# Reciprocal roots moved from GpSimd to VectorE, and the first layer's x scaled half on VectorE

## The chip, the cores and the metric

The kernel runs on one core of one Trainium2 chip. The metric is the device time of one execution in microseconds. Three runs of the kernel before gave 1405.43, 1406.83 and 1408.57 us, median 1406.83. The core has a matmul engine (TensorE, PE in the rows; PEld is its weight load), VectorE (DVE), ScalarE (ACT), GpSimd (POOL) and SyncE (SP, which issues all loads).

## What is computed

A trunk of two layers over 256 latent tokens and 256 context tokens of width 1024. The lines that matter here, cut from the reference:

```python
def rmsnorm(x, g):
    xf = x.astype(jnp.float32)
    y = xf * lax.rsqrt(jnp.mean(xf * xf, axis=-1, keepdims=True) + EPS)
    return (y * g.astype(jnp.float32)).astype(x.dtype)
...
for l in range(DEPTH):
    h = rmsnorm(x, norm_g[l, 0]) * (1.0 + mod[:, 1]) + mod[:, 0]
    y, yc = mixer_sublayer(h, hc, ...)
    x = x + mod[:, 2] * rmsnorm(y, norm_g[l, 1])
    h = rmsnorm(x, norm_g[l, 2]) * (1.0 + mod[:, 4]) + mod[:, 3]
    x = x + mod[:, 5] * rmsnorm(conv_ffn(h, ...), norm_g[l, 3])
...
```

In layer 0 the context tokens take the same steps. The mixer has four branches (mLSTM, differential attention, Fourier, spatial gating) with merge gates and one output projection; the FFN is gated, with a convolution over tokens. Each norm needs one reciprocal root for each token.

## The kernel before

All matmuls work on values split in a high and a low part (`hi`, `lo`), three matmuls for each product. `wload` (line 111) loads a weight tile of 128x1024, ScalarE casts it to `hi` (line 122), and `lo = raw - hi` is made on VectorE in one instruction or on GpSimd in four pieces of 128x256 (line 131), alternating by a running fraction. These subtractions are most of GpSimd's work.

Layer 0 keeps activations with the features on the partitions, in two halves of 256 tokens (context and latent). After the output projection and after the FFN's last matmuls, each half goes through `chain` (line 327). A column sum of squares over the tokens stands in PSUM (`st`); VectorE makes the variance from it (`rs_v`, line 176); `rsqrt` (line 149) raises it to the power -0.5 with one GpSimd instruction on a 128x2 tile (`rs_y`, line 151); and `spread_rows` (line 179) turns it with matmuls into a tile `R` that holds one root per column, in PSUM (line 182). Then VectorE scales y by R (line 341), VectorE and GpSimd add it to x (line 343), squares of the new x are summed, and the second norm repeats the same steps up to `modulate` (line 297, lines 300 to 302), which makes the next sublayer's input. There are four chains (two sublayers, two halves), so eight such roots. A chain is a generator: `pump` runs a step of it between groups of matmuls.

In layer 1 only the latent tokens go on, and the mixer's output is made with tokens on the partitions (`TokOut`): four quarters, two of tokens `t` by two of features `d`. `take` squares a quarter on ScalarE (line 439) and multiplies it by the gate row: on VectorE from PSUM (line 442), but for the last quarter (t = d = 1) by a ScalarE copy and a GpSimd product (lines 444 and 445; bit 1 of `yp`). `residual` makes the root for one token tile (`rstd_tok`, line 419, a 128x1 tile) and updates x (line 453). `tok_h1` squares the new x (line 483), multiplies it by the next norm's row (line 484), makes another root, scales the identity with it (`dg`, line 487), and TensorE turns the tokens back with `dg` (line 493), after which `tok_h2` splits h for the FFN. At the end of the FFN `residual(t, True)` also stores the result.

At the start of layer 0 (`start`), the norm's root comes last: matmuls run on unscaled x while the modulation is still being computed, then `R` is spread, VectorE copies it to SBUF (`Rs`, line 628), and GpSimd multiplies the eight tiles `x0[k]` (128x512) by it (line 631, `xr`). Then `bmain` interleaves steps of the modulation: matmuls `ada` (line 209), a VectorE copy of their result (`ada_sb`, line 213), small matmuls on that copy (line 219), and `shifted`, which makes the shifted h that the other branches read: a ScalarE pass (line 586), a VectorE pass `t` (line 587) and the low part (line 588).

Every engine works in its own fixed order. That order is made ahead of time by a planner that takes instructions by priority (the order of the program, moved by `later` and `issue_after`) as their inputs become ready by its own costs.

Of the kernel before, what the change touches and what calls it, by code (L numbers as in the profile page):

```python
# [10 lines left out]
F32 = mybir.dt.float32  # L11
F32R = mybir.dt.float32r
I32 = mybir.dt.int32
AF = mybir.ActivationFunctionType
ALU = mybir.AluOpType
# [7 lines left out]
KF = 22  # L23
EPS = 1e-6
SEGS = ((0, 6), (6, 14), (14, 22))
CFG = dict(hi=4, raw=4, tb=0.6, tw=0.8, tw1=1.0, x1=2, mm=3, paddk=8, tk=4, acc=2, f3=(2, 2), qa=(0, 0), f0=(1, 1), f1=(1, 2), f2=(1, 2), n0=(1, 1), n1=(1, 1), hd=1, hq=3, na=48, tu=3, to=1, ka=2, yp=3, ph=400, kh=4, kt=4, ld=2, dl=2, W=2, h0=3, mix=1, keep=4, hot=400, nst=6, nb=1, pt=(1, 0), w1=14, w2=6, wd=(24,), ahead={7: (0, -1, 1), 0: (2,), 1: (3,)}, so=("mddddfddd", "mdpf", "mpf", "mrpfd0q"), xr="pppppppp", fw=(0, 2), g0="nddddddd", g1=("nddddddn", "nddddddn"), g3=("nddddddn", "ndndndnd"), gy="nddddddn", cm=1, h1=2, xp=2, pf=(1, 1), ck=1, ys=(1, 1, 1, 1), c0=1, te=0.8)

C_ID, C_MF, C_MB, C_RC, C_RS, C_SEL, C_ONE, C_END = 0, 128, 256, 384, 448, 512, 514, 515
F_DFT, F_CD, F_SD, F_ND, F_END = 0, 512, 640, 768, 896
# [6 lines left out]
def trunk_kernel(ctx: ExitStack, tc: tile.TileContext, I, out):  # L36
    nc = tc.nc
# [3 lines left out]
    lp = ctx.enter_context(tc.tile_pool(name="lp", bufs=1))  # L41
    rawp = ctx.enter_context(tc.tile_pool(name="rawp", bufs=CFG["raw"]))
    hip = ctx.enter_context(tc.tile_pool(name="hip", bufs=CFG["hi"]))
    lop = ctx.enter_context(tc.tile_pool(name="lop", bufs=CFG["hi"]))
    hp = ctx.enter_context(tc.tile_pool(name="hp", bufs=1))
    tiny = ctx.enter_context(tc.tile_pool(name="tiny", bufs=4))
    wk = ctx.enter_context(tc.tile_pool(name="wk", bufs=2))
    zap = ctx.enter_context(tc.tile_pool(name="zap", bufs=1))
    mmp = ctx.enter_context(tc.tile_pool(name="mmp", bufs=CFG["mm"], space=PSUM))
    axp = ctx.enter_context(tc.tile_pool(name="axp", bufs=8 - CFG["mm"], space=PSUM))  # L50
    drp = ctx.enter_context(tc.tile_pool(name="drp", bufs=2, space=bass.MemoryType.DRAM))
# [7 lines left out]
    def aux(name="aux"):  # L59
        return axp.tile([128, 512], F32, tag="aux", name=name)  # L60
# [7 lines left out]
    def keep_warm(n, prev, mid=False):  # L68

        if n:  # L70
            ps = mmb("warm") if mid else aux("warm")
            with after(prev):
                for _ in range(2 * n):
                    at = nc.tensor.matmul(ps[:, 0:256], still[:, 0:128], still, start=True, stop=True)
            prev = ins_of(at)
        return prev

    turn = [0.0, CFG["tb"]]
    todo = []
# [69 lines left out]
    def rsqrt(v, n):  # L149
        y = tiny.tile([128, 16], F32, tag="rs_y", name="rs_y")[:, :n]  # L150
        nc.gpsimd.tensor_tensor(out=y, in0=v, in1=mh[:, :n], op=ALU.pow)
        return y

    @contextmanager
    def later(n):
        p = tc.cur_priority
        tc.cur_priority = p + n
        yield
        tc.cur_priority = p + (tc.cur_priority - p - n)

    def after(i):
        return tc.issue_after(i) if i is not None else ExitStack()
# [7 lines left out]
            nc.tensor.matmul(st[:, t:t + 1], sq[:, t * 128:(t + 1) * 128], onec, start=(first and t == 0),  # L170
                             stop=last and t == n // 128 - 1)

    def rstd_rows(st, n, spread=True):
        nt = n // 128
        v = tiny.tile([128, 16], F32, tag="rs_v", name="rs_v")[:, :nt]
        nc.vector.tensor_scalar(out=v, in0=st[:, :nt], scalar1=1.0 / D, scalar2=EPS, op0=ALU.mult, op1=ALU.add)
        return spread_rows(rsqrt(v, nt), nt) if spread else rsqrt(v, nt)

    def spread_rows(r, nt):
        R = aux("R")  # L180
        for t in range(nt):
            nc.tensor.matmul(R[:, t * 128:(t + 1) * 128], r[:, t:t + 1].to_broadcast([128, 128]), ident,
                             start=True, stop=True)
        return R[:, :nt * 128]
# [111 lines left out]
    def modulate(h, k, xk, R, c0, c1, A, B, boff):  # L296
        n = c1 - c0
        s = 0 if c0 == 0 else 1
        u = wk.tile([128, 512], F32, tag="t1", name="t1")
        nc.vector.scalar_tensor_tensor(out=u[:, :n], in0=xk, scalar=A[:, k, s:s + 1], in1=R, op0=ALU.mult, op1=ALU.mult)  # L300
        nc.scalar.activation(out=h[k][0][:, c0:c1], in_=u[:, :n], func=AF.Identity, bias=B[:, boff + k, s:s + 1], scale=1.0)  # L301
        nc.vector.scalar_tensor_tensor(out=h[k][1][:, c0:c1], in0=u[:, :n], scalar=B[:, boff + k, s:s + 1],
                                       in1=h[k][0][:, c0:c1].bitcast(F32), op0=ALU.add, op1=ALU.subtract)
# [24 lines left out]
    def chain(yn, c0, c1, G, h, A, B, boff, plan):  # L328

        n = c1 - c0  # L330
        s = 0 if c0 == 0 else 1
        r = rstd_rows(yn.acc[c0].st, n, False)
        for _ in range(CFG["ys"][0]):
            yield

        R = spread_rows(r, n // 128)
        S = Stat(n, plan)
        S.late = []
        for k in range(KD):
            t = yn.y[k][:, c0:c1]  # L340
            nc.vector.scalar_tensor_tensor(out=t, in0=t, scalar=G[:, k, s:s + 1], in1=R, op0=ALU.mult, op1=ALU.mult)
            e = nc.gpsimd if k < CFG["paddk"] and k % 2 == 0 else nc.vector
            e.tensor_tensor(out=x[c0][k], in0=x[c0][k], in1=t, op=ALU.add)
            S.drop(CFG["ys"][2])
            S.add(k, x[c0][k])
            if k % CFG["ck"] == CFG["ck"] - 1:
                yield

        for _ in range(CFG["ys"][3]):
            yield  # L350
        S.drop(0)

        r = rstd_rows(S.st, n, False)
        for _ in range(CFG["ys"][1]):
            yield

        R = spread_rows(r, n // 128)
        for k in range(KD):
            modulate(h, k, x[c0][k], R, c0, c1, A, B, boff)
            if k % CFG["cm"] == CFG["cm"] - 1:  # L360
                yield
# [54 lines left out]
            g.append(gt)  # L416
        return g

    def rstd_tok(ss):
        v = tiny.tile([128, 16], F32, tag="rs_v", name="rs_v")[:, 0:1]  # L420
        nc.vector.tensor_scalar(out=v, in0=ss[:, 0:1], scalar1=ss[:, 1:2], scalar2=D * EPS, op0=ALU.add, op1=ALU.add)
        return rsqrt(v, 1)

    class TokOut:
        def __init__(self, grow):
# [21 lines left out]

        def residual(self, t, store=False):

            r = rstd_tok(self.ss[t])  # L450
            for d in range(2):
                xd = xt[t][:, d * 512:(d + 1) * 512]
                nc.vector.scalar_tensor_tensor(out=xd, in0=self.ys[t, d], scalar=r, in1=xd, op0=ALU.mult, op1=ALU.add)
                if store:
                    nc.sync.dma_start(out=out[t * 128:(t + 1) * 128, d * 512:(d + 1) * 512], in_=xd)
# [21 lines left out]
    def tok_h1(t, xa, arow, hb):  # L477

        ss = tiny.tile([128, 2], F32, tag="ss", name="ss")
        for d in range(2):  # L480
            jk = wk.tile([128, 512], F32, tag="sq", name="jk")
            xd = xt[t][:, d * 512:(d + 1) * 512]
            sq.append(nc.scalar.activation(out=jk, in_=xd, func=AF.Square, accum_out=ss[:, d:d + 1]))
            nc.vector.tensor_tensor(out=xa[t][:, d * 512:(d + 1) * 512], in0=xd, in1=arow[d], op=ALU.mult)
        r = rstd_tok(ss)
        dg = wk.tile([128, 512], F32, tag="t2", name="dg")[:, 0:128]
        hb["dg"] = nc.vector.tensor_scalar(out=dg, in0=ident, scalar1=r, scalar2=RS, op0=ALU.mult, op1=ALU.mult)
        for d in range(2):
            ps = aux("hT")
            for j in range(4):  # L490
                k = 4 * d + j
                with after(warmed[0]):
                    at = nc.tensor.matmul(ps[:, j * 128:(j + 1) * 128], xa[t][:, k * 128:(k + 1) * 128], dg,
                                          start=True, stop=True)
            hb[t, d] = ps
        if t == 0:
            warmed[0] = keep_warm(CFG["w2"], ins_of(at), True)
# [15 lines left out]
    def start(stp):  # L513
# [5 lines left out]
        x0 = [stp.tile([128, T], F32, name=f"x0{k}") for k in range(KD)]  # L519
# [8 lines left out]
        Rs = stp.tile([128, T], F32, name="Rs")  # L528
# [72 lines left out]
        S = Stat(T, CFG["g0"])  # L601
# [9 lines left out]
        nb, rs = CFG["nb"], []  # L611
# [13 lines left out]
            for c in CFG["so"][j]:  # L625
                steps[c]()
        r = rs[0]
        nc.vector.tensor_copy(Rs, spread_rows(r, 4))
        nc.vector.tensor_copy(idr, cst[:, C_ID:C_ID + 36])
        for k in range(KD):  # L630
            (nc.gpsimd if CFG["xr"][k] == "p" else nc.vector).tensor_tensor(out=x0[k], in0=x0[k], in1=Rs, op=ALU.mult)

        def bstep(i):
            bmain(nb + i)
# [13 lines left out]
    def layer(l):  # L648
# [15 lines left out]
        with ExitStack() as es:  # L664
# [23 lines left out]
            def hot():  # L688
                return later(-CFG["hot"] if last else 0)
# [933 lines left out]
def ins_of(i):  # L1623
    return i.ins if hasattr(i, "ins") else i
# [79 lines left out]
```

## Time and profile before

| | |
|---|---|
| median of three runs | 1406.83 us (1405.43 to 1408.57) |
| profiled execution, its own time | 1407.98 us |
| span of that execution | 1406.2 us |
| mean granted TensorE clock | 0.983 |
| busy: PE, PEld | 1336.9 us, 1195.1 us |
| busy: DVE, ACT, POOL | 863.8 us, 621.6 us, 849.7 us |

The busy time of an engine counts its instructions from start to end, so an instruction that is held up while it runs counts as busy. A line of the timeline gives the start, the time up to the end of the last of the merged instructions, the engine, the line of the kernel, the operation, the tiles (written tile first), the shapes and the count. In square brackets stands the idle time of the engine before it, and what ended it.

### The profile page before, as it was taken

What the parts mean: (1) busy time and instruction counts of PE and PEld (TensorE: products, weight loads), DVE (VectorE), ACT (ScalarE), POOL (GpSimd) and SP (SyncE); (2) the same over time, 40 slices, a digit from 0 to 9 for tenths busy, and PEclk for the clock granted to TensorE, in tenths of its full rate; (3) what the DMA queues carried; (4) which work ended last, traced back from release to release, by engine and by line L of the source; (5) the groups of instructions that cost most, each with busy time, mean ns of one, the idle gap of its engine ahead of it and who ended that gap; (6) DMA issues with size and microseconds to landing.
All of it is one profiled execution on the core that took longest, in us unless ns stands there. A gap on an engine that the chain in (4) does not pass through costs nothing. (4 is left out here: it accounts for less than half of the span.)

```text
span 1406.2 us, 22765 instructions
## 1 busy us (share of the span) xinstructions
PE 1336.9 (95%) x8514; PEld 1195.1 (85%) x8514; DVE 863.8 (61%) x1554; ACT 621.6 (44%) x1098; POOL 849.7 (60%) x978
## 2 busy tenths in 40 slices
PE   8798999999999979999799999898999999899998
PEld 6597899888878979888688889897999998899997
DVE  4738766888777465599886553768847543532323
ACT  4435534444324445423231333466636545554443
POOL 1533234456764676567565546675556898689894
PEclk9999999999999999999899999999999999999999
DMA  9422223433443443466577443343324455355552
GB/s 347 137 77 81 69 105 106 135 120 140 160 162 107 147 151 114 138 227 211 195 253 270 155 160 106 116 135 104 108 76 135 147 164 184 123 184 200 183 181 75
DMA packets 61935, 210.55 MB, mean 150 GB/s; under 512 B 7145, under 2 KB 9729, under 8 KB 61569
## 3 DMA queue, kind: packets, MB, share of 16 engines
q1 hardware_dynamic: 61824, 209.10, 44.1%
q8 instruction: 67, 1.10, 0.3%
q14 instruction: 44, 0.35, 0.1%
HBM read 208.01 MB, written 1.06 MB: 149 GB/s over the span
## 5 line engine op out<-in xcount | busy, mean ns | idle before, releaser
L131 POOL TENSOR_TENSOR lo<-raw,hi 128x256 fp32r<-128x256 f32 x814 | 698.6, 890 | 392.2 <-ACT hi L122 373.9
L122 ACT CAST hi<-raw 128x1024 fp32r<-128x1024 f32 (+2 forms) x284 | 293.7, 1036 | 336.1 <-PE ua L136 76.6
L131 DVE TENSOR_TENSOR lo<-raw,hi 128x1024 fp32r<-128x1024 f32 (+2 forms) x79 | 122.3, 1548 | 89.6 <-ACT hi L122 89.5
L135 PE MATMUL gt<-hh,hi 128*128 128x512 f32 (+1 forms) x512 | 175.3, 342 | 1.0 <-DVE sig L782 1.0
L137 PE MATMUL gt<-hh,lo 128*128 128x512 f32 (+1 forms) x512 | 172.8, 338 | 0.6 <-POOL lo L131 0.6
L136 PE MATMUL gt<-hl,hi 128*128 128x512 f32 (+1 forms) x512 | 172.2, 336 | 0.0
L135 PE MATMUL ug<-hh,hi 128*128 128x256 f32 (+1 forms) x384 | 125.9, 328 | 10.4 <-DVE ca L1488 10.4
L232 DVE SCALAR_TENSOR_TENSOR ar<-ar,scb 128x1024 f32<-128x1024 f32 x80 | 122.4, 1534 | 15.6 <-DMA ar<-w_adaT 14.8
L136 PE MATMUL ug<-hl,hi 128*128 128x256 f32 (+1 forms) x384 | 125.5, 327 | 0.0
L135 PE MATMUL ua<-hh,hi 128*128 128x256 f32 (+1 forms) x384 | 124.3, 324 | 0.9 <-ACT hh L301 0.9
L137 PE MATMUL ug<-hh,lo 128*128 128x256 f32 (+1 forms) x384 | 125.1, 326 | 0.0
L136 PE MATMUL ua<-hl,hi 128*128 128x256 f32 (+1 forms) x384 | 124.0, 323 | 0.1
L137 PE MATMUL ua<-hh,lo 128*128 128x256 f32 (+1 forms) x384 | 123.8, 322 | 0.0
L137 PEld LDWEIGHTS gt<-hh,lo 128*128 128x128 f32 x512 | 96.6, 189 | 11.6 <-POOL lo L131 0.8
L135 PEld LDWEIGHTS gt<-hh,hi 128*128 128x128 f32 x512 | 96.7, 189 | 11.0 <-DVE sig L782 1.2
L136 PEld LDWEIGHTS gt<-hl,hi 128*128 128x128 f32 x512 | 96.8, 189 | 10.0
L135 PEld LDWEIGHTS ug<-hh,hi 128*128 128x128 f32 x384 | 74.2, 193 | 16.9 <-issue 8.5
L135 PE MATMUL o<-fh,hi 128*128 128x256 f32 (+1 forms) x240 | 81.0, 337 | 0.0
L136 PE MATMUL mm<-lo,hh 128*128 128x256 f32 x272 | 78.6, 289 | 2.4 <-DVE lo L131 2.4
L136 PE MATMUL o<-fl,hi 128*128 128x256 f32 (+1 forms) x240 | 80.5, 335 | 0.0
L137 PE MATMUL o<-fh,lo 128*128 128x256 f32 (+1 forms) x240 | 80.5, 335 | 0.0
L135 PEld LDWEIGHTS ua<-hh,hi 128*128 128x128 f32 x384 | 72.8, 190 | 7.6 <-ACT hh L301 1.1
(312 smaller groups left out, 3250.6 us busy)
## 6 DMA issues: line engine op xcount, KB each, us to landing
raw<-w_up SPq DMA_DIRECT2D x92, 512.0 KB, 4.0
ar<-w_adaT SPq DMA_DIRECT2D x80, 512.0 KB, 4.1
raw<-w_gate SPq DMA_DIRECT2D x64, 512.0 KB, 3.5
raw<-w_tm SPq DMA_DIRECT2D x24, 512.0 KB, 3.5
raw<-w_dr SPq DMA_DIRECT2D x22, 512.0 KB, 3.5
raw<-w_dn SPq DMA_DIRECT2D x20, 512.0 KB, 3.7
ada_w<-w_ada SPq DMA_DIRECT2D x16, 512.0 KB, 8.3
raw<-w_branch SPq DMA_DIRECT2D x16, 512.0 KB, 3.6
```

The costliest lines, as they stand in the source:

```text
L122: nc.scalar.copy(hi[:, :n], raw[:, :n])
L131: e.tensor_tensor(out=lo[:, s], in0=raw[:, s], in1=hi[:, s].bitcast(F32), op=ALU.subtract)
L135: nc.tensor.matmul(ps, a[0], b[0], start=start, stop=False)
L136: nc.tensor.matmul(ps, a[0], b[1], start=False, stop=False)
L137: return nc.tensor.matmul(ps, a[1], b[0], start=False, stop=stop)
L232: nc.vector.scalar_tensor_tensor(out=raw if st == ns - 1 else junk, in0=raw, scalar=0.5, in1=scb[:, st, :], op0=ALU.mult, op1=ALU.mult, ac ...
```

## The change

1. A new helper `rsqrt_v` computes the reciprocal root on VectorE with eight instructions: a start value from the bits of the number, and then two polynomial steps.
2. `rstd_rows` and `rstd_tok` take the root as an argument. `chain` uses `rsqrt_v` for both of its norms. `residual` uses it for the second token tile when it does not store; `tok_h1` for the second token tile. The other roots stay on GpSimd.
3. `yp` goes from 3 to 2: the last quarter of layer 1's mixer output is multiplied on VectorE from PSUM, like the others. The FFN's last quarter stays as it was.
4. In `start`, ScalarE makes the copy `Rs`. VectorE multiplies `x0[0]` to `x0[3]` by `R` in PSUM; GpSimd multiplies `x0[4]` to `x0[7]` by `Rs`, in two halves of 256 columns each.

```diff
-yp=3, xr="pppppppp"
+yp=2, xr="ddddpppp"
...
+    def rsqrt_v(v, n):
+        y = tiny.tile([128, 16], F32, tag="rs_y", name="rs_y")[:, :n]
+        q = tiny.tile([128, 16], F32, tag="rs_q", name="rs_q")[:, :n]
+        nc.vector.tensor_scalar(out=y.bitcast(I32), in0=v.bitcast(I32), scalar1=-0.5, scalar2=float(0x5F3759DF),
+                                op0=ALU.mult, op1=ALU.add)
+        nc.vector.tensor_tensor(out=q, in0=y, in1=y, op=ALU.mult)
+        nc.vector.tensor_tensor(out=q, in0=q, in1=v, op=ALU.mult)
+        nc.vector.scalar_tensor_tensor(out=q, in0=q, scalar=-10.0 / 3, in1=q, op0=ALU.add, op1=ALU.mult)
+        nc.vector.scalar_tensor_tensor(out=y, in0=q, scalar=5.0, in1=y, op0=ALU.add, op1=ALU.mult)
+        nc.vector.tensor_tensor(out=q, in0=y, in1=y, op=ALU.mult)
+        nc.vector.scalar_tensor_tensor(out=q, in0=q, scalar=-27.0 / 1024, in1=v, op0=ALU.mult, op1=ALU.mult)
+        nc.vector.scalar_tensor_tensor(out=y, in0=q, scalar=9.0 / 16, in1=y, op0=ALU.add, op1=ALU.mult)
+        return y
...
-    def rstd_rows(st, n, spread=True):
+    def rstd_rows(st, n, spread=True, root=None):
...
-        return spread_rows(rsqrt(v, nt), nt) if spread else rsqrt(v, nt)
+        y = (root or rsqrt)(v, nt)
+        return spread_rows(y, nt) if spread else y
...
-        r = rstd_rows(yn.acc[c0].st, n, False)
+        r = rstd_rows(yn.acc[c0].st, n, False, rsqrt_v)
...
-        r = rstd_rows(S.st, n, False)
+        r = rstd_rows(S.st, n, False, rsqrt_v)
...
-    def rstd_tok(ss):
+    def rstd_tok(ss, root=None):
...
-        return rsqrt(v, 1)
+        return (root or rsqrt)(v, 1)
...
-            r = rstd_tok(self.ss[t])
+            r = rstd_tok(self.ss[t], rsqrt_v if t and not store else None)
...
-        r = rstd_tok(ss)
+        r = rstd_tok(ss, rsqrt_v if t else None)
...
-        nc.vector.tensor_copy(Rs, spread_rows(r, 4))
+        R = spread_rows(r, 4)
+        nc.scalar.copy(Rs, R)
         nc.vector.tensor_copy(idr, cst[:, C_ID:C_ID + 36])
         for k in range(KD):
-            (nc.gpsimd if CFG["xr"][k] == "p" else nc.vector).tensor_tensor(out=x0[k], in0=x0[k], in1=Rs, op=ALU.mult)
+            if CFG["xr"][k] == "p":
+                for c in (0, 256):
+                    nc.gpsimd.tensor_tensor(out=x0[k][:, c:c + 256], in0=x0[k][:, c:c + 256], in1=Rs[:, c:c + 256],
+                                            op=ALU.mult)
+            else:
+                nc.vector.tensor_tensor(out=x0[k], in0=x0[k], in1=R, op=ALU.mult)
```

## Rows read from the trace of the kernel before

**Rows 1.** The page, busy time of each engine, share of the span, count.
```profile
PE 1336.9 (95%) x8514; PEld 1195.1 (85%) x8514; DVE 863.8 (61%) x1554; ACT 621.6 (44%) x1098; POOL 849.7 (60%) x978
```
**Rows 2.** Waits of PE: who waited for whom, us in total, times, longest.
```profile
PE R L182 <- POOL rs_y L151: 7.7, 4, 4.1
PE ada L219 <- DVE ada_sb L213: 6.2, 1, 6.2
PE hT L493 <- DVE dg L487: 4.8, 1, 4.8
...
PE ua L135 <- ACT hh L301: 0.9, 1, 0.9
```
**Rows 3.** Timeline, GpSimd and VectorE, mLSTM's denominator, 191 to 196 us.
```profile
191.86 2.09 POOL L131 TENSOR_TENSOR lo<-raw,hi 128x256 fp32r<-128x256 f32 x3
...
192.64 0.65 DVE L1132 SCALAR_TENSOR_TENSOR de<-de 128x4 f32<-128x4 f32 x1
193.32 0.65 DVE L1133 TENSOR_TENSOR de<-de,uem 128x4 f32<-128x4 f32 x1
...
194.87 0.17 DVE L1132 SCALAR_TENSOR_TENSOR de<-de 128x4 f32<-128x4 f32 x1
195.07 0.17 DVE L1133 TENSOR_TENSOR de<-de,uem 128x4 f32<-128x4 f32 x1
```
**Rows 4.** Timeline, VectorE and GpSimd, second root of the first chain.
```profile
490.02 13.80 POOL L131 TENSOR_TENSOR lo<-raw,hi 128x256 fp32r<-128x256 f32 x16
...
499.75 0.15 DVE L176 TENSOR_SCALAR rs_v<-st 128x2 f32<-128x2 f32 x1
...
503.79 0.69 POOL L151 TENSOR_TENSOR rs_y<-rs_v,mh 128x2 f32<-128x2 f32 x1
```
**Rows 5.** Timeline, VectorE, GpSimd and PE, same root in the FFN sublayer.
```profile
893.53 6.37 POOL L131 TENSOR_TENSOR lo<-raw,hi 128x256 fp32r<-128x256 f32 x8 [1.80 <-ACT hi L122]
...
897.20 0.15 DVE L176 TENSOR_SCALAR rs_v<-st 128x2 f32<-128x2 f32 x1
...
900.54 2.78 POOL L131 TENSOR_TENSOR lo<-raw,hi 128x256 fp32r<-128x256 f32 x4
...
900.62 1.22 PE L182 MATMUL R<-cst,rs_y 128*128 128x128 f32 x4 [3.09 <-POOL rs_y L151]
```
**Rows 6.** Timeline, VectorE and GpSimd, first root of the second half.
```profile
514.64 0.16 DVE L176 TENSOR_SCALAR rs_v<-st 128x2 f32<-128x2 f32 x1 [0.20 <-PE st L170]
...
515.55 3.24 POOL L131 TENSOR_TENSOR lo<-raw,hi 128x256 fp32r<-128x256 f32 x4
```
**Rows 7.** Timeline, VectorE and GpSimd, token-major end of layer 1's mixer.
```profile
1188.74 0.69 DVE L442 TENSOR_TENSOR yt<-ty,grow 128x512 f32<-128x512 f32 x1 [8.95 <-ACT jk L439]
...
1196.95 2.77 POOL L131 TENSOR_TENSOR lo<-raw,hi 128x256 fp32r<-128x256 f32 x4
...
1197.69 0.20 DVE L421 TENSOR_SCALAR rs_v<-ss 128x1 f32<-128x1 f32 x1
...
1200.27 2.89 DVE L453 SCALAR_TENSOR_TENSOR xt<-yt,rs_y,xt 128x512 f32<-128x512 f32 x2 [2.39 <-POOL rs_y L151]
...
1201.43 4.58 POOL L131 TENSOR_TENSOR lo<-raw,hi 128x256 fp32r<-128x256 f32 x4
...
1206.55 0.74 DVE L487 TENSOR_SCALAR dg<-cst,rs_y 128x128 f32<-128x128 f32 x1 [1.01 <-POOL rs_y L151]
```
**Rows 8.** Timeline, GpSimd and VectorE, start of layer 0, 36 to 55 us.
```profile
37.53 10.50 POOL L631 TENSOR_TENSOR x<-x,Rs 128x512 f32<-128x512 f32 x8 [9.26 <-DVE Rs L628]
...
41.25 3.98 DVE L587 TENSOR_SCALAR t<-x,ms,mod 128x256 f32<-128x256 f32 x3
45.16 3.42 DVE L588 TENSOR_TENSOR hl<-t,hh 128x512 fp32r<-128x512 f32 x2
48.50 0.41 DVE L213 COPY ada_sb<-ada 128x256 f32<-128x256 f32 x1
...
49.48 1.05 DVE L587 TENSOR_SCALAR t<-x,ms,mod 128x256 f32<-128x256 f32 x3
```

More of the change, by code (lines that the diff above doesn't have):

```diff
@@ L25 @@
 SEGS = ((0, 6), (6, 14), (14, 22))
-CFG = dict(hi=4, raw=4, tb=0.6, tw=0.8, tw1=1.0, x1=2, mm=3, paddk=8, tk=4, acc=2, f3=(2, 2), qa=(0, 0), f0=(1, 1), f1=(1, 2), f2=(1, 2), n0=(1, 1), n1=(1, 1), hd=1, hq=3, na=48, tu=3, to=1, ka=2, yp=3, ph=400, kh=4, kt=4, ld=2, dl=2, W=2, h0=3, mix=1, keep=4, hot=400, nst=6, nb=1, pt=(1, 0), w1=14, w2=6, wd=(24,), ahead={7: (0, -1, 1), 0: (2,), 1: (3,)}, so=("mddddfddd", "mdpf", "mpf", "mrpfd0q"), xr="pppppppp", fw=(0, 2), g0="nddddddd", g1=("nddddddn", "nddddddn"), g3=("nddddddn", "ndndndnd"), gy="nddddddn", cm=1, h1=2, xp=2, pf=(1, 1), ck=1, ys=(1, 1, 1, 1), c0=1, te=0.8)
+CFG = dict(hi=4, raw=4, tb=0.6, tw=0.8, tw1=1.0, x1=2, mm=3, paddk=8, tk=4, acc=2, f3=(2, 2), qa=(0, 0), f0=(1, 1), f1=(1, 2), f2=(1, 2), n0=(1, 1), n1=(1, 1), hd=1, hq=3, na=48, tu=3, to=1, ka=2, yp=2, ph=400, kh=4, kt=4, ld=2, dl=2, W=2, h0=3, mix=1, keep=4, hot=400, nst=6, nb=1, pt=(1, 0), w1=14, w2=6, wd=(24,), ahead={7: (0, -1, 1), 0: (2,), 1: (3,)}, so=("mddddfddd", "mdpf", "mpf", "mrpfd0q"), xr="ddddpppp", fw=(0, 2), g0="nddddddd", g1=("nddddddn", "nddddddn"), g3=("nddddddn", "ndndndnd"), gy="nddddddn", cm=1, h1=2, xp=2, pf=(1, 1), ck=1, ys=(1, 1, 1, 1), c0=1, te=0.8)
 C_ID, C_MF, C_MB, C_RC, C_RS, C_SEL, C_ONE, C_END = 0, 128, 256, 384, 448, 512, 514, 515
```

## The prediction

> **What bounds the kernel now.** I read the page's busy times first: TensorE (PE) works for 1336.9 of 1406.2 us and no other engine for much over 60% [rows 1]. So the time is TensorE's matmuls plus its idle 69.3 us, and an edit elsewhere counts only through those gaps. Second came TensorE's table of waits [rows 2]. Three of its lines touch code of this change: 7.7 us in four waits of the matmuls R for a reciprocal root that GpSimd (POOL) makes, 6.2 us in the first layer's start for a VectorE (DVE) copy, and 4.8 us before the last transposes for dg, which scales by such a root. Together that is 18.7 us, the most that can be won. Third, the timelines of VectorE and GpSimd around these waits, to see what the late engine was doing.
>
> **What a small VectorE instruction costs.** The new root is eight dependent instructions on a 128x2 tile (128x1 in the token-major part): one tensor_scalar, then seven with two SBUF operands. The nearest rows are the denominator's steps in the mLSTM: 128x4, two SBUF operands, dependent. Where GpSimd is idle one takes 0.17 us, and the next starts 0.20 us later. While GpSimd subtracts, which is 0.70 us per 128x256 piece (2.09 for three), the same lines take 0.65 us and start 0.68 us apart [rows 3]: one small instruction for each piece that GpSimd finishes. So eight cost 8 x 0.20 = 1.6 us beside an idle GpSimd and about 8 x 0.69 = 5.5 us beside a busy one. GpSimd's power costs 0.70 us plus the pieces queued before it. The change pays only where the queue before the power is longer than 0.9 us and GpSimd then falls idle. I take the blocked price wherever rows show pieces running. If the new instructions are never held, 1.6 us is the other end, which rival B carries.
>
> The Trainium skill speaks of this in its page SBUF — State Buffer, section Who interferes with whom: a VectorE instruction with two SBUF inputs and a GpSimd instruction that reads SBUF share one pair of ports, and whichever starts second is fully blocked until the other ends. Rows 3 agree for VectorE's side. By the rule GpSimd too would be held, by 0.17 us for each of the eight, 1.4 us per root; its pieces keep their 0.70 us in rows 3, so the sum has nothing for that, and by the rule it would be up to 1 us longer at each busy place.
>
> **Residual chains of layer 0, eight roots (two sublayers, two token halves, two norms).**
> - The second root of the first half. Its variance ends at 499.90, while GpSimd runs 16 pieces until 503.82, and the power lies behind them from 503.79 until 504.48 [rows 4]; this is TensorE's 4.1 us wait. On VectorE the 3.9 us until 503.8 let 5 to 6 small instructions through, and the other 2 or 3 go at 0.20: end at 504.2 to 504.4. Gain 0.2 us. The wait moves from one engine's queue to the other's port.
> - The same root in the FFN sublayer. Variance at 897.35; pieces run until 899.90, then the power, then from 900.54 four more pieces of 2.78 us [rows 5]. With the power gone these four follow at once, so GpSimd is busy until 902.7, 5.3 us, which is 7.7 small instructions: the root ends near 902.7 instead of 900.5. TensorE already waits there. Loss 2.1 us.
> - The first root of the second half in the mixer sublayer. Variance at 514.80, GpSimd idle, power at once, done when from 515.55 four pieces of 3.24 us begin [rows 6]. Without the power these pieces start sooner. Two small instructions pass, four or five are held, the rest go free: end near 518.5. R is next in TensorE's order, so it stands 2.9 us longer. Of this 0.9 us is a wait that comes soon after and goes (ua for hh) [rows 2]. Loss 2.0; bounds 0.8 (none held: 1.6 against 0.8) and 2.9.
> - The other five. Between them they have almost none of the 7.7 us, since the longest, 4.1, and the one at 900.62, 3.1, make up most of it [rows 2, 5], so TensorE had other work when their powers ended. That work is the cover. Free, each is 1.6 - 0.78 = 0.8 us later (0.70 for the power and 0.08 before it starts); held, up to 4.7. I take 0.3 each, 1.4 us in all (0 to 4).
> VectorE is in order, so the scalings of y and x by R and the adds that follow are queued behind the eight; they need R anyway. What else stands behind them, a conversion's second half or a weight subtract, waits 1.6 to 5.5 us and is inside the terms above.
>
> **Token-major end of layer 1's mixer.** The last quarter's gate product, before a ScalarE copy and a GpSimd multiply, becomes one VectorE instruction from PSUM, as the first quarter's at 1188.74, which took 0.69 us while GpSimd was subtracting [rows 7]. The variance of rs_v at 1197.69 is then ready near 1198.6. On GpSimd the power and the multiply go, and eight pieces run back to back from 1196.95 to about 1202.5 [rows 7]. That holds some six of the eight: root near 1202.9 against 1200.27, 2.6 us later. The two residual updates then meet an idle GpSimd: about 1.4 us, two at the 0.69 of the quarter, instead of 2.89 [rows 7], and the two products after them shrink alike, about 1 us. So the next variance is again near 1205.4. The second root is 1.6 us free against a wait of 1.0 [rows 7]: 0.6 late. If the ScalarE casts now queued behind the later squares release four pieces in that stretch, it is 3 late. Before the change 4.58 us of pieces stand just ahead of that root, so I take 2.0 us later for dg, the last thing that TensorE waits for there. Bounds: 3 later, and 2 earlier if the first root meets no pieces.
>
> **Start of layer 0.** Before: one VectorE copy of R to SBUF, then eight GpSimd products of 10.50 us in all. Beside them VectorE's shifts (t) take 3.98 us for three, against 1.05 in the next round, and its differences (hl) 3.42 for two, so that the copy TensorE waits for starts at 48.50 [rows 8]. After: ScalarE copies R. VectorE makes four products from PSUM, priced by the 128x512 product from PSUM that took 0.69 [rows 7]: 2.8 us, less the removed copy. GpSimd makes eight halves of 0.70: about 5.6 us, to near 43. Until then VectorE's small steps pay one half each (cast, shift, difference, shift: about 3.5 us from 40.1). After that the rest is free: two shifts 0.7, two differences at the 0.69 of a 128x512 product 1.4. The copy starts near 45.7, 2.8 us sooner, and what follows is a chain on VectorE and ScalarE, so the gain stays. The earlier copy of that kind, now behind the four products, is 1.4 us later, under the 6.2 us wait. Bounds: 5.3 if nothing is held, 0 if the halves hold as long as the whole tiles.
>
> **Sum.** -0.2 + 2.1 + 2.0 + 1.4 + 2.0 - 2.8 = 4.5 us longer. The profiled execution took 1407.98 us (span 1406.2), so 1412.5 by it. The median of the runs, 1406.83, is 1.15 lower, inside their spread, so the time I give is 1406.83 + 4.5 = 1411.3 us. Its own range is 1408 to 1418: all upper bounds together (+0 + 2.1 + 2.9 + 4 + 3 + 0) give 12, not likely all at once.
>
> **Rivals.**
> A, no change that can be measured: the losses at the third place, the five covered roots and dg fall under waits that come later, and only the two measured places and the start remain: -0.2 + 2.1 - 2.8 = -0.9, 1405.9 us. For it: most powers had cover. Against it: TensorE is 95% busy, and R stands in its order.
> B, faster: the eight instructions are not held, or GpSimd's pieces come in other places. Then the root is 1.6 us after its variance: 501.5 instead of 504.5 (-3.0), 899.0 instead of 900.5 (-1.5), dg 2 earlier, start 4 earlier, against +0.8 and +1.0 at the covered ones: -8.7, 1398.1 us. It decides from the point where eight take under 2.6 us beside pieces. Against it: rows 3, the same kind of instruction.
> C, the planner writes another order: R moves in TensorE's queue, or other VectorE work comes between the eight. The change then does not do what it says at these places, by some 3 us either way: 1404 to 1410.
>
> **Chances.** Forecast 0.54, A 0.22, B 0.18, C 0.06. Within 0.2% (2.8 us, about what a measurement here tells from none) is 1404.0 to 1409.6: A, a small part of the forecast and half of C, 0.27. Faster: B and part of C and A, 0.21. Slower: 0.52. The range goes down to 1399, into B, and up to 1418.
>
> **What would show it.** Right: at the roots near 500 and 897 the small instructions step 0.7 us apart beside the pieces, R starts near 504.3 and 902.7, a new wait of 2 to 3 us stands before R near 515, dg ends later than 1207.3, and the first copy wait falls from 6.2 to near 3.4 us. Wrong: the eight pass in 1.6 us beside running pieces, or TensorE's wait for R falls below 5 us in all; or the start gains nothing.

## The result and the profile after

The changed kernel took 1415.91 us (median of four runs, 1415.06 to 1418.74) against 1406.69 us for the kernel before on the same chip: a ratio of 1.0068 with a 95% interval of 1.0050 to 1.0086, 9.2 us longer. The profiled execution took 1415.06 us, its span 1413.3 us at a mean granted clock of 0.979. The forecast was 4.5 us longer.

The page's busy times of the changed kernel, as in [rows 1]:

```profile
PE 1340.4 (95%) x8514; PEld 1197.4 (85%) x8514; DVE 886.7 (63%) x1638; ACT 620.6 (44%) x1098; POOL 839.4 (59%) x967
```

VectorE gained 22.9 us, GpSimd lost 10.3. VectorE runs 84 instructions more, 80 of them the steps of ten roots.

TensorE's table of waits of the changed kernel (us in total, times, longest), as in [rows 2]:

```profile
PE ug L135 <- DVE ca L1509: 12.0, 4, 7.7
PE R L197 <- DVE rs_y L165: 9.8, 5, 3.7
PE hT L508 <- DVE dg L502: 8.4, 1, 8.4
...
PE ada L234 <- DVE ada_sb L228: 2.0, 1, 2.0
...
PE v L137 <- DVE hl L317: 1.5, 1, 1.5
PE ua L136 <- DVE hl L317: 1.5, 1, 1.5
```

Of the three lines that the change aims at, one fell and two grew: the copy in the start from 6.2 to 2.0, the roots R from 7.7 to 9.8, dg from 4.8 to 8.4. The waits for `hl`, the last step of `modulate`, are new: these two, and one of 0.6 at `f`.

Where the 9 us arise is read from the start times of the same matmul, counted in TensorE's order (8514 in each trace). Each number is its start in that trace less its start in the trace before, in us; e1 to e9 are the experiments below:

| matmul that started at | after | e1 start | e2 chains | e3 tokens | e7 yp | e9 chains, columns | e4 all, columns |
|---|---|---|---|---|---|---|---|
| 124.2 (start done) | -6.0 | -5.9 | +0.8 | +0.4 | +0.1 | -0.5 | -3.4 |
| 494.1 (first mixer done) | -5.2 | -5.7 | -0.8 | +0.4 | +0.3 | -0.5 | -3.6 |
| 560.0 (mixer's chains done) | -5.0 | -5.6 | -0.9 | 0.0 | +0.3 | -3.9 | -7.3 |
| 888.0 (FFN done) | -4.1 | -4.3 | -1.1 | +0.5 | -0.6 | -4.1 | -7.9 |
| 960.1 (FFN's chains done) | +2.2 | -3.8 | +7.0 | +0.5 | -0.7 | -3.7 | -7.5 |
| 1200.0 (layer 1's mixer done) | +2.6 | -2.1 | +9.2 | +2.0 | -0.7 | -2.5 | -6.3 |
| 1240.0 (token-major part done) | +7.1 | -2.4 | +9.3 | +6.9 | +2.1 | -1.5 | -5.2 |

In the changed kernel the start wins 6.0, the mixer's chains cost 0.2, the FFN's chains 6.3, the token-major part 4.4. Between them small parts come and go; the 1.1 to 2.2 us between 960 and 1200 in five of these traces stand where their edits change nothing, so single profiles differ by that much. They can differ by more: e1 and e10 below are one kernel, and the matmul that started at 41.9 us before comes 0.1 us sooner in e1 and 2.3 us later in e10; at 1240 us they are 5.1 us apart. So what a stage costs is read between two rows, from one profile each, and what a change is worth from the times.

### The profile page after: what moved, and what is told of

Its sections match the earlier page's. It is cut to its first block, busy times and chain, and to the rows that moved or that the text cites. A ratio compares the mean times of both kernels' runs of the same rounds, so it can differ in the third digit from the quotient of the medians.

```text
span 1413.3 us, 22835 instructions
## 1 busy us (share of the span) xinstructions
PE 1340.4 (95%) x8514; PEld 1197.4 (85%) x8514; DVE 886.7 (63%) x1638; ACT 620.6 (44%) x1098; POOL 839.4 (59%) x967
## 4 chain that ended last, share of the span: by engine, by line
PE 50%; DVE 6%; POOL 3%; issue 2%; DMA 1%; ACT 1%; DVEq 0%; ACTq 0%; SPq 0%; POOLq 0%
PE ug L135 4%; PE ug L136 4%; PE ug L137 4%; PE ua L135 4%; PE ua L136 4%; PE ua L137 4%; PE o L135 3%; PE o L136 3%; PE o L137 3%; POOL lo L131 2%; PE ty L135 2%; PE ty L136 2%; PE ty L137 2%; PE gt L137 2%; PE gt L135 2%; PE gt L136 2%
## 5 line engine op out<-in xcount | busy, mean ns | idle before, releaser
L137 PE MATMUL ug<-hh,lo 128*128 128x256 f32 (+1 forms) x384 | 124.2, 324 | 0.0
L135 PE MATMUL ua<-hh,hi 128*128 128x256 f32 (+1 forms) x384 | 124.2, 324 | 0.0
L136 PEld LDWEIGHTS ua<-hl,hi 128*128 128x128 f32 x384 | 72.7, 190 | 8.2 <-DVE hl L317 1.7
```

Source lines behind the costliest of these rows:

```text
L135: nc.tensor.matmul(ps, a[0], b[0], start=start, stop=False)
L136: nc.tensor.matmul(ps, a[0], b[1], start=False, stop=False)
L137: return nc.tensor.matmul(ps, a[1], b[0], start=False, stop=stop)
```

## The experiments

Each run is compared with the kernel before on the same chip (medians there 1409.77 us for e1 to e4, 1410.46 for e5 to e8, 1408.06 for e9 to e11). The theory H is that small VectorE instructions are held while GpSimd's pieces run, as the prediction priced them; its rival O needs no such holding.

### e1: the start alone

```diff
-xr="pppppppp"
+xr="ddddpppp"
-        nc.vector.tensor_copy(Rs, spread_rows(r, 4))
+        R = spread_rows(r, 4)
+        nc.scalar.copy(Rs, R)
... (the products as in the change; all roots and yp as before)
```

> Only the start's part of the change (ScalarE copy of R, four products on VectorE from PSUM, eight halves on GpSimd); all roots and the last quarter stay on GpSimd. In the changed kernel the waits that follow the start come 6.0 us earlier than before (128.18 to 122.16). Theory H (parts add up; the loss sits in the roots): 6.0 us under before, about 1400.7. Rival O (the gain was luck of order and is given back later by waits on loads): within 2.5 us of before.

Measured: 1405.62 us, ratio 0.9976 (0.9967 to 0.9986), 3.4 us faster by the ratio, between the 6.0 of H and the 2.5 of O. At 124 us it is 5.9 ahead, but 1.3 of it goes between 560 and 888, where one more wait of `ug` for `ca` appears, and more later. The start is a gain, though less in the time than at its own place.

### e2: the eight chain roots alone

```diff
-        r = rstd_rows(yn.acc[c0].st, n, False)
+        r = rstd_rows(yn.acc[c0].st, n, False, rsqrt_v)
...
-        r = rstd_rows(S.st, n, False)
+        r = rstd_rows(S.st, n, False, rsqrt_v)
```

> Only the eight roots of the residual chains on VectorE, all else as before. Theory H (each small VectorE instruction with two SBUF operands waits for one GpSimd piece): the lag between the landmarks at 128 and 962 us of the two traces grew by 8.1 us, so about 8 us over before, near 1414.8, and the roots at about 500 and 897 us take 4 to 5 us each. Rival O (the loss is the planner's other order and TensorE's lower clock in longer stretches): less than 4 us over before, under 1411, with the same 4 to 5 us roots.

Measured: 1416.44 us, 1.0054 (1.0042 to 1.0065), 7.6 us slower, as by H. In the trace 8.1 us are lost between 888 and 960, in the FFN's chains, and none in the mixer's.

### e3: the two token-major roots and yp

```diff
-yp=3
+yp=2
-            r = rstd_tok(self.ss[t])
+            r = rstd_tok(self.ss[t], rsqrt_v if t and not store else None)
...
-        r = rstd_tok(ss)
+        r = rstd_tok(ss, rsqrt_v if t else None)
```

> Only the token-major part: two roots on VectorE and the last quarter's product on VectorE. The landmarks around it (1165 and 1220 us) moved apart by 4.4 us. Theory H: about 4.4 us over before, near 1411; dg ends some 3.5 us later, and TensorE's wait for it grows from 4.8 to about 8.4 us. Rival O: within 2 us of before.

Measured: 1414.78 us, 1.0034 (1.0022 to 1.0046), 4.8 us slower; TensorE's wait for dg is 8.4 us, as in the changed kernel and as by H. The three parts give -3.4 + 7.6 + 4.8 = 9.0, so they add up to the change.

### e4: all ten roots in a form that isn't held

The steps become tensor_scalar instructions on one column each, with the other factors as per-partition scalars: 14 for a 128x2 tile, 7 for 128x1. No instruction has two SBUF tensors. All else is the changed kernel.

```diff
-        nc.vector.tensor_tensor(out=q, in0=y, in1=y, op=ALU.mult)
-        nc.vector.tensor_tensor(out=q, in0=q, in1=v, op=ALU.mult)
+        for c in cs:
+            ts(out=q[:, c], in0=y[:, c], scalar1=y[:, c], scalar2=v[:, c], op0=ALU.mult, op1=ALU.mult)
... (the other steps alike)
```

> The changed kernel with the same root in another form: one column at a time, 128x1 tensor_scalar instructions with pointer scalars (14 for two tokens' columns, 7 for one), so that no instruction has two SBUF tensors. It keeps every root on VectorE and issues more instructions there. Theory H: 128x1 tensor_scalars were not held before (0.20 us beside running pieces), so a root takes 1.4 to 2.5 us even beside pieces; TensorE's wait for R at 499 us falls to about 1.5 us, dg comes some 5 us earlier, and the whole is 1398 to 1404. Rival O (it is the work and the order on VectorE, not the port): at or over the changed kernel, 1414 or more.

Measured: 1402.41 us, 0.9951 (0.9940 to 0.9963): 6.9 us faster than before, where the change was 9 slower. The timeline of VectorE and GpSimd of this kernel at the second root of the first chain, the place of [rows 4]:

```profile
486.47 14.10 POOL L131 TENSOR_TENSOR lo<-raw,hi 128x256 fp32r<-128x256 f32 x15
...
496.13 0.15 DVE L199 TENSOR_SCALAR rs_v<-st 128x2 f32<-128x2 f32 x1
496.32 0.21 DVE L161 TENSOR_SCALAR rs_q<-rs_v 128x1 int32<-128x1 int32 x2
496.51 0.45 DVE L164 TENSOR_SCALAR rs_q<-rs_q,rs_v 128x1 f32<-128x1 f32 x2
...
497.93 0.33 DVE L174 TENSOR_SCALAR rs_y<-rs_q 128x1 f32<-128x1 f32 x2
498.18 1.78 DVE L131 TENSOR_TENSOR lo<-raw,hi 128x1024 fp32r<-128x1024 f32 x1
```

Pieces run from 486.47 to 500.57, over the whole root, and fourteen instructions end 1.98 us after the variance; the eight of the change took 4.35 at this place (below). TensorE's waits for R and dg in this kernel:

```profile
PE hT L517 <- DVE dg L511: 4.7, 1, 4.7
...
PE R L206 <- DVE rs_y L174: 2.5, 2, 1.7
```

H holds and O falls: the roots on the same engine beside running pieces lose nothing once the form isn't held. The token-major part shows it best: there e4 has the changed kernel's 16 pieces in a row (from 1190.64, 12.83 us), the first root takes 1.74 us instead of 4.69, and the wait for dg is 4.7 instead of 8.4.

### e9: the chain roots alone in that form

> The eight chain roots alone, on VectorE in the one-column form (128x1 tensor_scalar steps); start and token-major part as in the kernel before. With the eight-instruction form of the change these same roots alone came out at 1.0054 of the kernel before, 7.6 us slower. Theory that the held steps make that loss: the one-column roots take about 2 us beside pieces, TensorE's wait for R falls from 7.7 to about 2.5 us, and the time is 3.5 to 5 us shorter, 0.997. Rival, the move to VectorE itself costs (other VectorE work comes between the steps, the scalings behind it wait): then the loss remains in part, 0 to 4 us slower, 1.000 to 1.003.

Edit: e2 with the steps of e4. Measured: 1405.19 us, 0.9986 (0.9972 to 1.0001), 2.0 us faster, against 7.6 slower in e2: 9.6 us for the form alone. The time gain is under the 3.5 to 5 expected, although the trace is 3.7 ahead at 960; the rest is lost behind it, where this edit changes nothing.

### e7: yp alone

```diff
-yp=3
+yp=2
```

> The kernel before with one edit: yp from 3 to 2 (the last quarter of layer 1's mixer output is multiplied by VectorE from PSUM); all roots stay on GpSimd. The token-major part of the change alone came out 4.8 us slower, with TensorE's wait for dg at 8.4 us against 4.8 before. Theory T1, the held roots on VectorE make that loss: without them the quarter is ready no later than before, so this kernel is within 1 us of the one before and the wait for dg stays between 4 and 6 us. Theory T2, the freed ScalarE makes it: with its copy gone, ScalarE casts three weight tiles in a row, GpSimd gets 16 pieces back to back, and whatever root or update stands there is late; then this kernel is 3 to 5 us slower, with the wait for dg at 7 us or more and the powers queued behind pieces. I take T2, at 0.55, 3 us slower.

Measured: 1410.09 us, 1.0000 (0.9991 to 1.0008); T2, which I had taken, falls in its size. T1 has the time right, but the wait for dg is 6.4, over its 4 to 6. GpSimd's timeline and TensorE's wait for dg in this kernel:

```profile
1196.27 2.80 POOL L131 TENSOR_TENSOR lo<-raw,hi 128x256 fp32r<-128x256 f32 x4
1199.02 0.55 POOL L151 TENSOR_TENSOR rs_y<-rs_v,mh 128x1 f32<-128x1 f32 x1
1199.54 7.30 POOL L131 TENSOR_TENSOR lo<-raw,hi 128x256 fp32r<-128x256 f32 x8
1206.80 0.55 POOL L151 TENSOR_TENSOR rs_y<-rs_v,mh 128x1 f32<-128x1 f32 x1
```
```profile
PE hT L493 <- DVE dg L487: 6.4, 1, 6.4
```

With the copy gone, pieces fill the place (eight after the first power, where [rows 7] have four), the second power waits behind them, and the wait for dg grows by 1.6. The median doesn't show it. So nearly all of e3's 4.8 us come with the two roots on VectorE. Whether the eight-instruction root would cost as much there with yp=3, no run shows.

### e6: all roots in columns, yp back to 3

Edit: e4 with yp=3.

> The changed kernel with all ten roots in the one-column form, and yp back to 3 (ScalarE copies the last quarter, GpSimd multiplies it). Under T2 (the freed ScalarE lets 16 pieces run back to back) the copy puts the casts back behind the squares, so the two residual updates and the two products meet fewer pieces and dg comes 1 to 2 us sooner than with yp=2: 0.994 of the kernel before. Under T1 only the form of the roots mattered, and the quarter is now later by a copy and a GpSimd product: the same as with yp=2 or up to 1.5 us slower, 0.995 to 0.996.

Measured: 1404.07 us, 0.9945 (0.9931 to 0.9960), not to be told from e4. The copy did not put the casts back: ScalarE still casts three tiles in a row, and twelve pieces run through the two updates, so the missing copy is not what lines up the casts. What yp does is then worth nothing that can be measured.

### e8, e10: the start with whole tiles, and with halves again

```diff
-                for c in (0, 256):
-                    nc.gpsimd.tensor_tensor(out=x0[k][:, c:c + 256], in0=x0[k][:, c:c + 256], in1=Rs[:, c:c + 256],
-                                            op=ALU.mult)
+                nc.gpsimd.tensor_tensor(out=x0[k], in0=x0[k], in1=Rs, op=ALU.mult)
```

> The start part alone, as in the run of that part (VectorE makes four products from PSUM, ScalarE copies R), but GpSimd multiplies its four x tiles whole, 128x512, four instructions in place of eight halves. The theory that a small VectorE step waits for the GpSimd instruction that runs when it starts: a held step then costs up to 1.31 us in place of 0.70, some three steps are held, so the copy that TensorE waits for comes 1 to 2 us later than with halves, TensorE's wait for ada_sb is 3 to 4 us against 2.0, and the time is 1 to 2 us longer than that of the start part, some 2 us faster than before. Rival, the halves do nothing and the gain is only the shared work: copy and time the same as the start part within 0.5 us, some 4 us faster than before.

> The start part alone with GpSimd's products in halves, as run before (0.9976), now on the chip and in the hour of the kernels beside it; with whole tiles it gave 0.9956. If the halves and the whole tiles are the same and the difference is that of two sessions, this gives 0.996 to 0.997 (4 to 6 us faster); if whole tiles are better by themselves, it stays at 0.9976 (3.4 us faster). The copy that TensorE waits for starts 6.6 to 7.0 us after VectorE's first product, in either case, as it did with halves (6.96) and with whole tiles (6.75).

Measured: whole tiles 1403.88 us, 0.9956 (0.9943 to 0.9970); halves again 1404.71 us, 0.9976 (0.9963 to 0.9989), the ratio of e1. The copy that TensorE waits for starts 6.75 us after VectorE's first product with whole tiles, 6.96 and 6.97 with halves: a held step costs more, but fewer are held, and the holding theory's 1 to 2 us don't come. The gain is the shared work; by time, whole tiles are not worse, and whether they are better by themselves stays open.

### e5, e11: start and chain roots in columns, tokens as before

> The start part as in the change, the eight chain roots on VectorE in the one-column form (128x1 tensor_scalar steps), and the token-major part as in the kernel before (powers on GpSimd, yp=3). If the token-major part costs nothing once its roots are in columns, this is as fast as the kernel with all ten roots in columns, 0.995 of the kernel before, 1402 to 1403 us. If yp=2 still costs there (that run stood 6.3 us ahead of the kernel before at 1190 us and 5.2 ahead at 1220), this is 1 us faster than that, 0.994. I take 0.994.

> The start part with GpSimd's four products whole, the eight chain roots on VectorE in the one-column form, the token-major part as in the kernel before. If halves and whole tiles are the same, this is 0.994 to 0.9945, as with halves; if whole tiles are better by themselves by the 2.8 us between the two start runs, it is 0.992 to 0.9925, 10 to 11 us faster than the kernel before. I take 0.994.

Edit: e1 and e9 together, with halves (e5) or whole tiles (e11). Measured: 1402.87 us, 0.9944 (0.9932 to 0.9957), and 1400.89 us, 0.9942 (0.9924 to 0.9961). These are the fastest versions: by the ratios some 8 us below the kernel before, and 17 to 18 below the change. Leaving the token-major part on GpSimd neither adds nor takes anything measurable against e4.

## Why the prediction was right, and where not

The direction and the reason were right: small instructions, seven of the eight with two SBUF inputs, don't pass beside pieces. The terms, with the five covered roots' 1.4 spread evenly:

| term | predicted | in the trace after | the part alone, by time |
|---|---|---|---|
| start | -2.8 | -6.0 | -3.4 (e1, e10) |
| mixer's chains | -0.2 + 2.0 + 0.6 | +0.2 | |
| FFN's chains | 2.1 + 0.8 | +6.3 | +7.6 both (e2) |
| token-major | +2.0 | +4.4 | +4.8 (e3) |

That the trace's four stages sum to 4.9, close to the 4.5, is luck: the start gained 3.2 more than forecast and the mixer's chains cost 2.2 less, the FFN's chains 3.4 more and the token-major part 2.4 more. By time the forecast was too small by half: the chains by 2.3, the token-major part by 2.8. Of the signs named, the steps near 500 and 897 came 0.7 apart, and R started at 499.10 and 898.08, which is 504.3 and 902.1 when what the trace was ahead is added; the wait before R near 515 did not come, and the copy's wait fell to 2.0 instead of 3.4.

**The held step: right.** The timeline after, VectorE, GpSimd and PE, at the place of [rows 4]:

```profile
487.44 11.10 POOL L131 TENSOR_TENSOR lo<-raw,hi 128x256 fp32r<-128x256 f32 x13
...
494.45 0.15 DVE L190 TENSOR_SCALAR rs_v<-st 128x2 f32<-128x2 f32 x1
494.63 0.52 DVE L157 TENSOR_SCALAR rs_y<-rs_v 128x2 int32<-128x2 int32 x1
495.19 0.65 DVE L159 TENSOR_TENSOR rs_q<-rs_y 128x2 f32<-128x2 f32 x1
...
497.91 0.65 DVE L163 TENSOR_TENSOR rs_q<-rs_y 128x2 f32<-128x2 f32 x1
498.59 0.16 DVE L164 SCALAR_TENSOR_TENSOR rs_q<-rs_q,rs_v 128x2 f32<-128x2 f32 x1
498.79 0.16 DVE L165 SCALAR_TENSOR_TENSOR rs_y<-rs_q,rs_y 128x2 f32<-128x2 f32 x1
499.10 1.19 PE L197 MATMUL R<-cst,rs_y 128*128 128x128 f32 x4 [3.68 <-DVE rs_y L165]
```

Six steps start 0.56 to 0.69 apart until the pieces end at 498.54, and the last two 0.20. The root takes 4.35 us; it ends 4.50 after the variance began, where the power ended 4.73 after it [rows 4]. That is the 0.2 won. The same root in the FFN took 4.91 us, 5.35 forecast. The rule that GpSimd too would be held, from the Trainium skill's page SBUF — State Buffer, Who interferes with whom, doesn't show for these small steps: four pieces beside held steps in the FFN take 2.77 us from 895.83, 0.69 each.

**First root of the mixer's second half: the place was wrong.** The timeline after, there, as in [rows 6]:

```profile
509.80 0.16 DVE L190 TENSOR_SCALAR rs_v<-st 128x2 f32<-128x2 f32 x1
510.38 2.80 POOL L131 TENSOR_TENSOR lo<-raw,hi 128x256 fp32r<-128x256 f32 x4 [1.03 <-ACT hi L122]
...
512.44 1.02 DVE L317 SCALAR_TENSOR_TENSOR hl<-t,mod,hh 128x256 fp32r<-128x256 f32 x1
...
513.51 0.39 PE L136 MATMUL ua<-hl,hi 128*128 128x256 f32 x1 [1.51 <-DVE hl L317]
...
514.62 0.16 DVE L165 SCALAR_TENSOR_TENSOR rs_y<-rs_q,rs_y 128x2 f32<-128x2 f32 x1
514.93 0.68 PE L197 MATMUL R<-cst,rs_y 128*128 128x128 f32 x4
```

The root took 4.82 us, where 3.7 were priced, since other VectorE work stands between its steps. But R had been moved back in TensorE's order and waits for nothing: rival C, at this place. The wait came at the first half's `hl` instead, which stands between the held steps: 1.51 us, against the 0.9 that went [rows 2]. The same half's second root, one of the five covered, was not covered: it took 3.58 us, and R waited 1.59 for it at 533.72, 0.14 before.

**FFN's chains: the term of the covered roots was too small, and the clock was left out.** TensorE's waits after, in the FFN's second half (idle time and its end in brackets):

```profile
914.08 0.38 PE L405 MATMUL f<-hi,hl 128*128 128x256 f32 x1 [0.58 <-DVE hl L317]
915.37 0.68 PE L197 MATMUL R<-cst,rs_y 128*128 128x128 f32 x4 [0.78 <-DVE rs_y L165]
920.26 0.58 PE L184 MATMUL st<-one,sq 128*128 128x1 f32 x4 [0.41 <-DVE sq L300]
931.83 0.68 PE L197 MATMUL R<-cst,rs_y 128*128 128x128 f32 x4 [1.75 <-DVE rs_y L165]
945.56 0.40 PE L137 MATMUL v<-hi,hl 128*128 128x272 f32 x1 [1.54 <-DVE hl L317]
946.89 0.40 PE L135 MATMUL v<-hi,hh 128*128 128x272 f32 x1 [0.54 <-ACT hh L316]
```

They sum to 5.60 us. In the trace before, the same stretch has three, 0.56 for `sq`, 2.01 for `ft` and 0.24 for a root: 2.81. The two roots took 4.49 and 3.17 us, inside the bounds given for a covered root; the value taken for it, 0.3, had rested on work of TensorE that covers the power but not three more microseconds. The last two waits are not the held root's: two late `hl` of `modulate`, before at 941.25, now start at 945.04, behind the spatial gating's work on VectorE, but `v` waits in e4 as well, where no root on VectorE is held and R waits for none in this half:

```profile
935.89 0.39 PE L137 MATMUL v<-hi,hl 128*128 128x272 f32 x1 [1.05 <-DVE hl L326]
...
937.22 0.40 PE L135 MATMUL v<-hi,hh 128*128 128x272 f32 x1 [0.54 <-ACT hh L325]
```

That is rival C again, another order on VectorE that comes with the move.

The clock adds to the first half. One stretch after, and two before, from the windows (us, busy time and instructions of PE, PEld, DVE, ACT, POOL, then the granted clock, and the DMA's share and GB/s):

```profile
891.92:904.19 12.27, 10.30 (x48) 10.04 (x49) 8.70 (x19) 4.06 (x8) 6.59 (x11) 0.50 0.45 154
```
```profile
900.62:904.28 3.66, 3.66 (x17) 3.66 (x18) 2.33 (x5) 0.91 (x2) 2.71 (x4) 0.53 0.43 143
904.28:908.37 4.09, 4.09 (x38) 4.09 (x37) 3.41 (x8) 2.68 (x5) 1.59 (x3) 1.00 0.37 128
```

Around this root TensorE is at its lower level, 1.2 GHz (granted clock 0.50), for 12 us after and, once its wait is over, 3.5 us before; after, it fell in the second of two waits for squares (their matmuls start at 888.85 and 891.04), and stayed down through the wait for R. At the upper level 38 matmuls take 4.09, so by estimate 48 would take 5.2 instead of 10.30, some 5.1 us lost, and before 17 would take 1.8 instead of 3.66, 1.8 lost. The wait for R is 1.1 shorter, one for squares 0.2. So 3.3 - 1.1 - 0.2 = 2.0 in the first half, which is what its matmuls are later by when it ends. The second half makes the other 4.2; the waits explain 2.8 of it, and 1.4 stay open. In e2 the lower level lasts 4.5 us behind the wait for R, that wait is longer, 4.67, and the stage costs 8.1: the held root costs as much without the long low stretch. In e4 and e9 the stage costs 0.4.

**Token-major part: eight pieces were counted, sixteen came.** The timeline after, as in [rows 7]:

```profile
1199.59 12.77 POOL L131 TENSOR_TENSOR lo<-raw,hi 128x256 fp32r<-128x256 f32 x16
1199.65 2.93 ACT L122 CAST hi<-raw 128x1024 fp32r<-128x1024 f32 x3
...
1200.92 0.20 DVE L436 TENSOR_SCALAR rs_v<-ss 128x1 f32<-128x1 f32 x1
...
1205.17 0.65 DVE L165 SCALAR_TENSOR_TENSOR rs_y<-rs_q,rs_y 128x1 f32<-128x1 f32 x1
1205.85 2.31 DVE L468 SCALAR_TENSOR_TENSOR xt<-yt,rs_y,xt 128x512 f32<-128x512 f32 x2
1208.09 2.34 DVE L499 TENSOR_TENSOR xa<-xt,grow 128x512 f32<-128x512 f32 x2
...
1213.19 0.29 DVE L502 TENSOR_SCALAR dg<-cst,rs_y 128x128 f32<-128x128 f32 x1
```

The first root takes 4.69 us, 4.3 forecast. Then the forecast has GpSimd idle, updates of 1.4 and products 1 us shorter. But ScalarE casts three tiles in a row, where before two casts stood behind the late squares, and the pieces run on to 1212.36. That the missing copy makes it so is not shown: with the copy back, e6 casts three in a row too. The updates take 2.31, the products 2.34, and the second root 2.61 instead of 1.6. Counted from where this part begins, 2.6 us later than before, dg ends 3.6 later, where 2.0 were forecast; the case of 3 was named and not taken. The pieces by themselves don't cost this: in e4 the same 16 run, the updates take 1.89 and the products 2.34, the roots 1.74 each, and dg ends 0.2 sooner than before, counted alike.

**Start: right in kind, too small.** The timeline after, as in [rows 8]:

```profile
37.08 5.59 POOL L649 TENSOR_TENSOR x<-x,Rs 128x256 f32<-128x256 f32 x8 [9.16 <-ACT Rs L644]
37.03 2.48 DVE L652 TENSOR_TENSOR x<-x,R 128x512 f32<-128x512 f32 x4 [2.87 <-ACT Rs L644]
...
39.95 0.63 DVE L594 CAST Bh<-mod 128x4 fp32r<-128x4 f32 x1
40.50 0.90 DVE L602 TENSOR_SCALAR t<-x,ms,mod 128x256 f32<-128x256 f32 x1
41.32 0.68 DVE L595 TENSOR_TENSOR Bl<-mod,Bh 128x4 fp32r<-128x4 f32 x1
41.92 1.54 DVE L602 TENSOR_SCALAR t<-x,ms,mod 128x256 f32<-128x256 f32 x3
43.39 0.68 DVE L603 TENSOR_TENSOR hl<-t,hh 128x512 fp32r<-128x512 f32 x1
43.99 0.41 DVE L228 COPY ada_sb<-ada 128x256 f32<-128x256 f32 x1
```

The copy starts 6.96 us after the first product, 10.97 before [rows 8] and 8.2 by the forecast. The products from PSUM take 0.62 each beside GpSimd's products, so they aren't held; the steps that are cost less than four halves; and the copy was placed ahead of the second `hl`, 0.6 sooner. From 42 us to the matmuls behind this copy all eight traces of this start (after, e1, e4, e5, e6, e8, e10, e11) gain 4.2 to 4.5. After and in e1, e5 and e6 another 1.5 follow, which are the clock: before, TensorE, idle for 6.2 us, ran from 48.96 to 54.20 at a granted clock of 0.50; after, with a wait of 1.97, at 1.00 from 44.46 to 55.00. In e4, e8, e10 and e11 the lower level came here all the same, for 3.4 us, and only 0.2 to 0.3 follow. That, and what is given back later, lies between the 6.0 of the trace and the 3.4 of the time.

**What didn't decide.** Rival A needed the covered roots to stay covered. Rival B decides from the point where a root passes beside pieces in under 2.6 us; the eight took 4.35 and 4.91, but the one-column form took 1.98 and 2.24, and the kernel then went B's way: 6.9 us faster, against B's 8.7. Rival C's other order came at two places, the moved R and the late `hl`, but the time lies outside its 1404 to 1410.

## What to carry to other kernels

Before moving a chain of small instructions to VectorE, look whether GpSimd streams beside it, and write the chain so that no step has two SBUF tensors and each has one column: here it was then not held, though it has nearly twice as many instructions. Price a covered step by how long the cover lasts beyond it, not by its old end, and count anew what will run in the same stretch. A wait just ahead of a long run of matmuls can cost twice, once as idle time and once at the lower clock; behind the wait of 2.0 us in the start the clock stayed up in four of the traces and was down for 3.4 us in the others.

## What the runs showed of the hardware

- The form decides which small instruction is held beside 128x256 subtractions on GpSimd. Held: 128x2 or 128x1 with two SBUF tensors (0.65 us), tensor_scalar on 128x2 int32 (0.52 above), a cast of 128x4 (0.63 above). Not held: tensor_scalar on 128x1, 0.14 to 0.16 us with constants, 0.21 with one and 0.27 with two per-partition scalars, beside pieces as without them; the variance from PSUM, 0.15; and a 128x512 product with one input in PSUM, 0.62. The Trainium skill's page SBUF — State Buffer (Who interferes with whom) says so: with at most one SBUF input and outside the two-port modes VectorE doesn't meet GpSimd, and cast and tensor_scalar can enter such a mode. The traces agree: 0.65 us with two SBUF tensors, 0.15 to 0.27 with one column of one. The Trainium skill's page VectorE: DVE Perf Modes (Mode 2×_2P) splits the access pattern for that mode in half along its outermost dimension. That a single column leaves nothing to split is my reading; 0.52 held on 128x2 and 0.15 on 128x1 fit it, but no run shows the mode itself.
- A one-column step with two per-partition scalars does the work of two tensor steps at 0.27 us, so seven free steps for one column end in 1.74 us, and fourteen for two columns in 1.98.
